# A two-layer hybrid trunk on one core: the norms' inverse root on GpSimd, later transposes, low parts by accumulating DMAs, and a shared end

## The chip, the cores and the metric

The kernel runs on one core of a Trainium2 chip. The metric is the time of one execution on the device in microseconds (us). The engines are named as in the profile: PE is TensorE's matmul, PEld its weight load, DVE is VectorE, ACT is ScalarE, POOL is GpSimd, SP is SyncE, whose queue starts most of the DMAs. "Issue" means that an engine's queue starts a DMA, "landing" that its last byte is written.

## The reference

The input `x` is 512 tokens of 1024 numbers in float32. Two layers follow each other; each has a token mixer and a gated feed-forward part, and each of these four parts ends in a residual sum and a layer norm:

```python
for i in range(DEPTH):                                  # DEPTH = 2
    if i % 3 == 0: y = gla_mixer(h, ...)                # gated linear attention (layer 0)
    elif i % 3 == 1: y = gdn_mixer(h, ...)              # gated DeltaNet (layer 1)
    h = layer_norm(ALPHA * h + y, ln_g[i, 0], ln_b[i, 0])
    h = layer_norm(ALPHA * h + conv_ffn(h, ...), ln_g[i, 1], ln_b[i, 1])

def layer_norm(x, g, b):
    mu = mean(x, -1); var = mean(square(x - mu), -1)
    return (x - mu) * rsqrt(var + 1e-5) * g + b

def conv_ffn(x, w_in, conv_w, w_out):                   # w_in: 1024 x 5632, w_out: 2816 x 1024
    gate, up = split(causal_dwconv(x @ w_in, conv_w), 2)
    return (gelu(gate, approximate=False) * up) @ w_out
```

## The kernel before

All matrix products are made in three terms: each operand is split into a high part in the format fp32r and a low part, the remainder, and TensorE adds high x high, high x low and low x high (`tm_terms`, and `fm_mms` for products whose result lies transposed). The high part of a weight is a cast on ACT (`wsh`, `wh`), the low part a subtraction on DVE (`wsl<-raw,wsh`, `wl<-raw,wh`). For some weights (`plan_fm(..., bydma=True)`) the low part is instead made by ACT, which writes minus the rounded weight, and by a DMA from POOL's queue that adds the raw weight to it (L315 to L317).

The tokens are four blocks of 128 (`tb` 0 to 3). The residual stream is kept as eight tiles `h[tb][hf]` of 128 tokens by 512 features, the halves `hf` 0 and 1. At the end of each of the four parts, a block's projection adds to `h`, `bn_stats` takes the statistics of both halves, and the norm follows: `ln_stats` makes the mean and variance (`ln_mv`, `ln_var`), a first guess of the inverse root by integer arithmetic on its bits (the seed, L680), and three Newton rounds of two steps each (L683, L684: `ln_t`, `ln_rs`). `ln` then makes `ln_nb` = -mean x root, scales one half on ACT (L697) and the other on DVE (L698), and TensorE transposes both (`tr4`, `xT`, L172). ACT takes the transposed tiles out with the norm's factors (`xf`), and they are split in high and low parts (`xh`, `xl`) that the next part's products read. There are 16 such norms: four blocks after GLA's output projection, after the first FFN, after GDN's output projection and at the end. The last four go through `ln_out` instead, which applies the norm's factors by two DVE operations per half (L747, L748) and writes the output by SP's queue.

An FFN computes its output projection in parts: most of it in Strassen-like sums while the input products run, and the rest, the last 512 of the 2816 rows, in `last_proj`: eight weights of 128 x 512 held in slots (`wsh`, `wsl`), eight output tiles (`tm`) of four chunks, three products each. The fourth chunk's other operand is the last gate times up value of the FFN, which ACT casts to `gh` and DVE completes to `gl`.

The program is written out as one stream for all engines. `clk` is a planner's count of TensorE's time, `vec` one of DVE's; tasks (`spawn`, `pump`) are resumed when `clk` reaches their due time, so that work of one block is put between the products of another. The instructions of an engine keep the scheduler's order; what `keep_in_program_order` is given stays where it is written. Raw weights go through three buffers (`RAWB = 3`), loaded by SP's queue in the order of a plan; a buffer can be loaded anew when whoever reads it has finished. `look` sets how many weights ahead are cast; the letter `l` in an FFN's `order` raises it for the last projection's weights:

```python
self.fm_items(items, steps, order[:-4] + "l" + order[-4:] if plain else order)
```

Of the kernel before, what the change touches and what calls it, by code (L numbers as in the profile page):

```python
# [8 lines left out]
F32 = mybir.dt.float32  # L9
# [3 lines left out]
AF = mybir.ActivationFunctionType  # L13
ALU = mybir.AluOpType

P = 128
D = 1024
S = 512
# [23 lines left out]
INV_DELAY = 18.0  # L42
CONV_DELAY = 6.0
COLS_DELAY = 64.0
BASE_PACE = 1.8
# [7 lines left out]
def blk(i, n=P):  # L53
    return slice(i * n, i * n + n)


class Trunk:
# [97 lines left out]

    def mm(self, out, a, b, start=True, stop=True, open_group=False):
        n = 1
        for d in b.shape[1:]:
            n *= d
        self.clk += n * (0.00045 if b.dtype == F32R else 0.00175)  # L160
        t = self.nc.tensor.matmul(out, a, b, start=start, stop=stop, skip_group_check=open_group)  # L161
        if self.pin:
            self.tc.keep_in_program_order(t)
# [5 lines left out]

    def tr(self, out, a, n=P):  # L170
        self.clk += 0.11
        t = self.nc.tensor.transpose(out, a, self.ident[:n, :n])  # L172
        if self.pin:
            self.tc.keep_in_program_order(t)

    def tr4(self, out, a):
        for j in range(4):
            self.tr(out[:, blk(j)], a[:, blk(j)])

# [92 lines left out]
    def issue(self, item):  # L272

        nc = self.nc
# [27 lines left out]
        if self.in_slots(item):  # L302
            w = []
            for j in range(used // S):
                wh, wl = self.slot("wsh", F32R), self.slot("wsl", F32R)
                nc.scalar.copy(wh, raw[:, blk(j, S)])
                nc.vector.tensor_sub(wl, raw[:, blk(j, S)], wh)
                self.vec(0.7)
                w.append((wh, wl))
            return w  # L310
# [115 lines left out]

    def tm_terms(self, ps, ah, al, wh, wl, first, last):
        self.mm(ps, ah, wh, first, False)
        self.mm(ps, ah, wl, False, False)
        self.mm(ps, al, wh, False, last)  # L430

# [238 lines left out]
    def ln_stats(self, tb):  # L670
# [11 lines left out]
        for _ in range(3):  # L682
            nc.vector.scalar_tensor_tensor(t, rs, hv, rs, ALU.mult, ALU.mult)  # L683
            nc.vector.scalar_tensor_tensor(rs, t, 1.5, rs, ALU.subtract, ALU.mult)  # L684
        self.vec(2.0)
        return mv, rs

    def ln(self, tb, spill=False):
# [10 lines left out]
        ready = self.vec(0.65)  # L699
        yield ready - self.clk + 0.2  # L700
        for hf in range(2):
            ps = self.psum("xT")
            self.tr4(ps, h[hf])
            xf = self.slot("xf")
# [37 lines left out]
    def ln_out(self, tb, out):  # L742
        nc = self.nc
        gb, h = self.ln_gb(), self.h[tb]
        mv, rs = self.ln_stats(tb)
        for hf in range(2):
            nc.vector.scalar_tensor_tensor(h[hf], h[hf], mv[:, 0:1], gb[hf], ALU.subtract, ALU.mult)  # L747
            nc.vector.scalar_tensor_tensor(h[hf], h[hf], rs, gb[2 + hf], ALU.mult, ALU.add)  # L748
            nc.sync.dma_start(out[blk(tb), blk(hf, S)], h[hf])
        yield 0.0  # L750
# [31 lines left out]
    def ffn_plan(self, w_in, w_out):  # L782
# [10 lines left out]
        for hf in range(2):  # L793
            for f in range(2 * p0, 2 * p1, 2):
                self.plan_tm(w_out, f * P, 2, hf * S, True)

# [21 lines left out]
    def ffn(self, cw, li, g, b, final, out=False):  # L818
# [3 lines left out]
        for p0, p1 in CHUNKS + (PLAIN,):  # L822
# [3 lines left out]
            for f in range(2 * p0, 2 * p1):  # L826
# [17 lines left out]
                items += [gate, up]  # L844
            self.fm_items(items, steps, order[:-4] + "l" + order[-4:] if plain else order)
            steps = self.sums_proj(xs, p0 == 0)
# [7 lines left out]
    def last_proj(self, xs, final):  # L854
# [739 lines left out]
```

## Time and profile before

| | us |
|---|---|
| three runs | 1286.13, 1277.92, 1284.02 |
| their median | 1284.02 |
| profiled execution | 1284.87 |
| its span, first to last instruction | 1283.2 |
| PE busy in it | 1258.0 (98%) |
| DVE busy | 872.2 (68%) |
| ACT busy | 611.3 (48%) |
| POOL busy | 152.2 (12%) |
| mean granted TensorE clock | 0.984 of full speed |

The span is what the trace covers; the device's time is 1.7 us longer. An engine's share is its busy time over the span. In the rows below, a timeline row has the start in us, the duration, the engine, the line, the operation with out<-in, and in brackets the idle time before it with its releaser. A row of waits has the engine and line that waited, the one that released it, the total, the number of waits and the longest. A row of a group has the count, then the busy time and the mean in ns. A row of DMA issues has the queue, the count, the size of each and the median us from issue to landing. A row of a stretch has its bounds, its length, the busy time of PE, PEld, DVE, ACT and POOL with the number of instructions, and at its end the granted clock, the DMA share and GB/s.

### The profile page before, as it was taken

The numbers are of one execution on the slowest core, as the hardware profiler recorded it, in microseconds if no ns is written. First come the engines' busy times: TensorE is split into PE (matmuls) and PEld (weight loads), VectorE is DVE, ScalarE is ACT, GpSimd is POOL, SyncE is SP. The second block draws the span as 40 slices with busy tenths as digits, with TensorE's granted clock in tenths as the row PEclk, the third lists the DMA queues.
The fourth block names the chain that finished last, engine by engine and source line by source line (L and its number), as shares of the span: only waits on it lengthen the run. The fifth ranks groups of instructions, "written<-read, shape, count | busy, mean of one in ns | idle before, by whom it ended". The sixth has DMA issues, their size and how long they took to land.

```text
span 1283.2 us, 17783 instructions
## 1 busy us (share of the span) xinstructions
PE 1258.0 (98%) x6558; PEld 1060.1 (83%) x6558; DVE 872.2 (68%) x1704; ACT 611.3 (48%) x1176; POOL 152.2 (12%) x226
## 2 busy tenths in 40 slices
PE   8999999999999999999999999999999999999996
PEld 6878888988888888879888889988898888888885
DVE  3683366578666666686789925668877766766678
ACT  3553443644544444435765525544554554554440
POOL 4000000012201201101112210100002211211200
PEclk9999999999999999999999959999999999999998
DMA  6422224078757757641444411333239766766821
GB/s 183 116 69 65 66 95 136 17 155 214 170 127 182 162 128 176 148 134 66 128 125 110 125 37 35 99 103 95 82 99 212 159 157 160 161 153 150 211 82 65
DMA packets 182646, 159.07 MB, mean 124 GB/s; under 512 B 18328, under 2 KB 141786, under 8 KB 182560
## 3 DMA queue, kind: packets, MB, share of 16 engines
q1 hardware_dynamic: 161728, 114.05, 30.1%
q0 software_dynamic: 19440, 42.06, 17.8%
q10 hardware_dynamic: 1392, 1.84, 0.4%
q8 instruction: 51, 0.84, 0.3%
q14 instruction: 35, 0.29, 0.1%
HBM read 141.65 MB, written 5.78 MB: 115 GB/s over the span
## 4 chain that ended last, share of the span: by engine, by line
PE 82%; DVE 7%; DMA 2%; ACT 1%; issue 1%; SPq 0%; DVEq 0%; ACTq 0%; POOLq 0%
PE fm L161 43%; PE tm L161 29%; PE o L161 2%; PE R L161 1%; PE V L161 1%; DMA wq<-in_ffn_w_out_dram 1%; PE xT L172 1%; DVE conv L1166 1%; DVE wl L322 1%; PE pg L161 1%; PE vn L161 1%; PE yT L172 1%; PE qkT L172 1%; PE s L161 0%; PE qs L161 0%
## 5 line engine op out<-in xcount | busy, mean ns | idle before, releaser
L161 PE MATMUL fm<-xh,wh 128*128 128x512 f32 (+1 forms) x1104 | 409.2, 371 | 0.4 <-ACT wh L321 0.4
L161 PE MATMUL fm<-xl,wh 128*128 128x512 f32 (+1 forms) x1104 | 405.5, 368 | 0.0
L161 PE MATMUL fm<-xh,wl 128*128 128x512 f32 (+1 forms) x1096 | 401.7, 368 | 2.4 <-DVE wl L322 2.4
L322 DVE TENSOR_TENSOR wl<-raw,wh 128x1024 fp32r<-128x1024 f32 (+1 forms) x134 | 162.6, 1215 | 142.1 <-ACT wh L321 139.0
L161 PEld LDWEIGHTS fm<-xh,wh 128*128 128x128 f32 x1104 | 209.6, 190 | 34.2 <-ACT wh L321 1.2
L161 PEld LDWEIGHTS fm<-xh,wl 128*128 128x128 f32 x1096 | 207.8, 190 | 36.3 <-DVE wl L322 3.0
L161 PEld LDWEIGHTS fm<-xl,wh 128*128 128x128 f32 x1104 | 209.8, 190 | 32.7
L321 ACT CAST wh<-raw 128x1024 fp32r<-128x1024 f32 (+1 forms) x134 | 139.7, 1043 | 200.8 <-PE fm L161 107.9
L815 DVE SCALAR_TENSOR_TENSOR conv<-fm,ffn_cw,conv 128x511 f32<-128x511 f32 (+1 forms) x176 | 131.1, 746 | 16.5 <-ACT conv L813 14.5
L266 ACT CAST wh<-wq 128x512 fp32r<-128x512 f32 x126 | 74.7, 619 | 110.9 <-DMA wq<-in_ffn_w_out_dram 37.5
L267 DVE TENSOR_TENSOR wl<-wq,wh 128x512 fp32r<-128x512 f32 x126 | 84.9, 687 | 61.8 <-ACT wh L266 61.3
L224 POOL DMA_DIRECT2D wq<-in_ffn_w_out_dram x72 | 63.0, 901 | 263.2 <-DVE wl L267 150.2
L161 PE MATMUL tm<-wh,gh 128*128 128x512 f32 x216 | 84.4, 391 | 0.3 <-DVE h L521 0.3
L161 PE MATMUL tm<-wl,gh 128*128 128x512 f32 x216 | 84.2, 390 | 0.0
L161 PE MATMUL tm<-wh,gl 128*128 128x512 f32 x216 | 84.2, 390 | 0.0
L161 PE MATMUL tm<-wh,xh 128*128 128x512 f32 x192 | 79.6, 415 | 1.0 <-ACT qk L982 1.0
L161 PE MATMUL tm<-wh,xl 128*128 128x512 f32 x192 | 75.5, 393 | 0.0
L161 PE MATMUL tm<-wl,xh 128*128 128x512 f32 x192 | 75.2, 391 | 0.0
L317 POOL DMA_DIRECT2D wl<-raw x20 | 17.5, 875 | 442.0 <-ACT wl L316 425.4
L521 DVE TENSOR_TENSOR h<-h,tm 128x512 f32<-128x512 f32 x68 | 44.9, 683 | 34.8 <-PE tm L161 34.8
L813 ACT ACTIVATE conv<-fm,ffn_cw 128x512 f32<-128x512 f32 x88 | 59.7, 681 | 0.0
L1166 DVE SCALAR_TENSOR_TENSOR conv<-fm,gdn_cw,conv 128x509 f32<-128x509 f32 (+2 forms) x72 | 53.4, 744 | 4.6 <-ACT conv L1164 4.1
(297 smaller groups left out, 1877.4 us busy)
## 6 DMA issues: line engine op xcount, KB each, us to landing
raw<-in_ffn_w_in_dram SPq DMA_DIRECT2D x88, 512.0 KB, 4.9
wq<-in_ffn_w_out_dram SPq DMA_DIRECT2D x72, 256.0 KB, 5.9
wq<-in_ffn_w_out_dram POOLq DMA_DIRECT2D x72, 256.0 KB, 5.2
raw<-in_gdn_w_in_dram SPq DMA_DIRECT2D x32, 512.0 KB, 4.1
raw<-in_gla_w_in_dram SPq DMA_DIRECT2D x23, 512.0 KB, 3.7
wl<-raw POOLq DMA_DIRECT2D x20, 512.0 KB, 4.8
raw<-in_gla_w_out_dram SPq DMA_DIRECT2D x8, 512.0 KB, 3.7
h<-in_ln_b_dram POOLq DMA_DIRECT2D x16, 256.0 KB, 7.3
```

What stands on the lines that cost most here:

```text
L161: t = self.nc.tensor.matmul(out, a, b, start=start, stop=stop, skip_group_check=open_group)
L172: t = self.nc.tensor.transpose(out, a, self.ident[:n, :n])
L224: nc.gpsimd.dma_start(t[i], quad(i, r, col), accum_op=ALU.add)
L266: nc.scalar.copy(wh, t)
L267: nc.vector.tensor_sub(wl, t, wh)
L317: nc.gpsimd.dma_start(wl.bitcast(F32), raw, accum_op=ALU.add)
L321: nc.scalar.copy(wh[:, cols], raw[:, cols])
L322: nc.vector.tensor_sub(wl[:, cols], raw[:, cols], wh[:, cols])
L521: nc.vector.tensor_tensor(h, h, banks[bank][j], op)
L813: nc.scalar.activation(a, ps, AF.Identity, scale=tap(2))
L815: nc.vector.scalar_tensor_tensor(a[:, d:], ps[:, :S - d], tap(2 - d), a[:, d:], ALU.mult, ALU.add)
L1166: self.conv = nc.vector.scalar_tensor_tensor(a[:, d:], ps[:, :S - d], tap(3 - d), a[:, d:], ALU.mult, ALU.add)
```

## The change

Three parts. The norms: the three Newton rounds go to GpSimd, as three operations each instead of two; the planner counts 0.5 instead of 2.0 for DVE; a norm's transposes become due `LN_LAG` = 2.7 after DVE's planned end instead of 0.2, and are pinned in program order, as are the last projection's products (`tr`, `tr4` and `tm_terms` hand the new argument `order` on to `mm`'s condition). The last projection: the low parts of its weights are made by ACT and an accumulating DMA of POOL's queue; the lookahead is raised eight letters before the end of `order` instead of four. The end: for blocks 0 and 1, `ln_out` normalises on ACT, multiplies on DVE and adds `ln_b` by an accumulating DMA.

```diff
+LN_LAG = 2.7
...
-    def mm(self, out, a, b, start=True, stop=True, open_group=False):
+    def mm(self, out, a, b, start=True, stop=True, open_group=False, order=False):
...
-        if self.pin:
+        if self.pin or order:
             self.tc.keep_in_program_order(t)
...
     def issue(self, item):
...
                 nc.scalar.copy(wh, raw[:, blk(j, S)])
-                nc.vector.tensor_sub(wl, raw[:, blk(j, S)], wh)
-                self.vec(0.7)
+                if item[5] > 1:
+                    nc.scalar.mul(wl, raw[:, blk(j, S)], -1.0)
+                    nc.gpsimd.dma_start(wl.bitcast(F32), raw[:, blk(j, S)], accum_op=ALU.add)
+                else:
+                    nc.vector.tensor_sub(wl, raw[:, blk(j, S)], wh)
+                    self.vec(0.7)
...
     def ln_stats(self, tb):
...
         for _ in range(3):
-            nc.vector.scalar_tensor_tensor(t, rs, hv, rs, ALU.mult, ALU.mult)
-            nc.vector.scalar_tensor_tensor(rs, t, 1.5, rs, ALU.subtract, ALU.mult)
-        self.vec(2.0)
+            nc.gpsimd.tensor_mul(t, rs, rs)
+            nc.gpsimd.tensor_scalar(t, t, hv, 1.5, op0=ALU.mult, op1=ALU.subtract)
+            nc.gpsimd.tensor_mul(rs, rs, t)
+        self.vec(0.5)
...
     def ln(self, tb, spill=False):
...
-        yield ready - self.clk + 0.2
+        yield ready - self.clk + LN_LAG
         for hf in range(2):
             ps = self.psum("xT")
-            self.tr4(ps, h[hf])
+            self.tr4(ps, h[hf], True)
...
     def ln_out(self, tb, out):
...
         mv, rs = self.ln_stats(tb)
+        if tb < 2:
+            nb = self.small([P, 1], "ln_nb")
+            nc.vector.scalar_tensor_tensor(nb, mv[:, 0:1], -1.0, rs, ALU.mult, ALU.mult)
+            for hf in range(2):
+                nc.scalar.activation(h[hf], h[hf], AF.Identity, bias=nb, scale=rs)
+                nc.vector.tensor_mul(h[hf], h[hf], gb[hf])
+                nc.gpsimd.dma_start(h[hf], self.gb_rows[1][blk(hf, S)].partition_broadcast(P), accum_op=ALU.add)
+                nc.sync.dma_start(out[blk(tb), blk(hf, S)], h[hf])
+            return
         for hf in range(2):
             nc.vector.scalar_tensor_tensor(h[hf], h[hf], mv[:, 0:1], gb[hf], ALU.subtract, ALU.mult)
...
     def ffn_plan(self, w_in, w_out):
...
-                self.plan_tm(w_out, f * P, 2, hf * S, True)
+                self.plan_tm(w_out, f * P, 2, hf * S, 2)
...
     def ffn(self, cw, li, g, b, final, out=False):
...
-            self.fm_items(items, steps, order[:-4] + "l" + order[-4:] if plain else order)
+            self.fm_items(items, steps, order[:-8] + "l" + order[-8:] if plain else order)
...
     def last_proj(self, xs, final):
...
-                    self.tm_terms(ps, *(t[:, blk(tb)] for t in xs[c]), *ws[hf][c], c == 0, c == n - 1)
+                    self.tm_terms(ps, *(t[:, blk(tb)] for t in xs[c]), *ws[hf][c], c == 0, c == n - 1, True)
```

In the changed kernel the lines stand some further down: TensorE's products are at L162 and its transposes at L173, the Newton steps at L688 to L690, `ln_nb` at L702, the scalings at L703 and L704. Three places of the order follow, a row for an instruction, with its line, operation, out<-in and what it waits for.

DVE behind GDN's output projection, before: the seed of block 1 (`ln_rs_8208`) and the end of both blocks' Newton rounds, with `ln_nb` and the scaling of block 0 between them.

```order
L680 TENSOR_SCALAR ln_rs_8208<-ln_var_8206 128x1 [waits DVE_49]
L684 SCALAR_TENSOR_TENSOR ln_rs_8165<-ln_t_8166,ln_rs_8165 128x1 [waits DVE_49]
L683 SCALAR_TENSOR_TENSOR ln_t_8209<-ln_rs_8208,ln_var_8206 128x1 [waits DVE_49]
L696 SCALAR_TENSOR_TENSOR ln_nb_8174<-ln_mv_8161,ln_rs_8165 128x1 [waits DVE_49]
L698 TENSOR_SCALAR h_7863<-h_7863,ln_mv_8161,ln_rs_8165 128x512
```

DVE at the same place in the changed kernel, from block 0's seed (`ln_rs_8197`) to block 1's scaling (`h_7897`).

```order
L685 TENSOR_SCALAR ln_rs_8197<-ln_var_8195 128x1 [waits DVE_49]
L474 SCALAR_TENSOR_TENSOR h_7907<-h_7907,tm_8116 128x512 [waits PE_49]
L702 SCALAR_TENSOR_TENSOR ln_nb_8209<-ln_mv_8193,ln_rs_8197 128x1 [waits Pool_49]
L704 TENSOR_SCALAR h_7895<-h_7895,ln_mv_8193,ln_rs_8197 128x512
L481 BN_STATS ln_st_8093<-h_7907 128x6 [waits DVE_49]
L678 BN_AGGR ln_mv_8239<-ln_st_8093 128x2 [waits DVE_49]
L680 TENSOR_SCALAR ln_var_8241<-ln_mv_8239 128x1 [waits DVE_49]
L685 TENSOR_SCALAR ln_rs_8243<-ln_var_8241 128x1 [waits DVE_49]
L702 SCALAR_TENSOR_TENSOR ln_nb_8255<-ln_mv_8239,ln_rs_8243 128x1 [waits Pool_49]
L704 TENSOR_SCALAR h_7897<-h_7897,ln_mv_8239,ln_rs_8243 128x512
```

Block 1's statistics and seed moved from before block 0's `ln_nb` to behind it, and each `ln_nb` now waits for POOL.

PE at the same place, before: the second half of block 0 (`h_7873`), and the products up to block 1's first half (`h_7865`).

```order
L172 MATMUL xT_8257<-ident_80,h_7873 128x128 [waits Activation_49]
L172 MATMUL xT_8257<-ident_80,h_7873 128x128 x3
L161 MATMUL tm_8086<-wsh_7997,yh_7739 128x512
L161 MATMUL tm_8086<-wsl_7998,yh_7739 128x512
L161 MATMUL tm_8086<-wsh_7997,yl_7740 128x512
L161 MATMUL tm_8086<-wsh_8001,yh_7739 128x512
L161 MATMUL tm_8086<-wsl_8002,yh_7739 128x512
L161 MATMUL tm_8086<-wsh_8001,yl_7740 128x512
L172 MATMUL xT_8294<-ident_80,h_7865 128x128 [waits DVE_49]
```

PE there in the changed kernel, where the two halves are `h_7905` and `h_7897`.

```order
L162 MATMUL tm_8117<-wsh_8135,yl_7975 128x512
L173 MATMUL xT_8295<-ident_80,h_7905 128x128 [waits Activation_49]
L173 MATMUL xT_8295<-ident_80,h_7905 128x128 x3
L173 MATMUL xT_8307<-ident_80,h_7897 128x128 [waits DVE_49]
L173 MATMUL xT_8307<-ident_80,h_7897 128x128 x3
L162 MATMUL tm_8118<-wsh_8029,yh_7771 128x512
```

The six products that stood between the two halves now stand behind both; the transposes of blocks 2 and 3 moved to later places.

ACT at the end of the first FFN, before: the last of its weights' casts, then casts of GDN's first weights (`wh`) around `gh`.

```order
L306 CAST wsh_4713<-raw_4711 128x512 [waits DMAHW7_49]
L306 CAST wsh_4717<-raw_4711 128x512
L813 ACTIVATE conv_4774<-fm_4743,ffn_cw_28_176 128x512 [waits PE_49]
L321 CAST wh_4739<-raw_4737 128x1024 [waits DMAHW0_49]
L321 CAST wh_4770<-raw_4768 128x1024 [waits DMAHW1_49]
L563 CAST gh_4779<-conv_4774 128x512 [waits DVE_49]
L321 CAST wh_4797<-raw_4795 128x1024 [waits DMAHW2_49,PE_49]
L321 CAST wh_4811<-raw_4809 128x1024 [waits DMAHW3_49,PE_49]
```

ACT there in the changed kernel.

```order
L307 CAST wsh_4726<-raw_4724 128x512 [waits DMAHW7_49]
L309 ACTIVATE wsl_4727<-raw_4724 128x512
L307 CAST wsh_4731<-raw_4724 128x512
L309 ACTIVATE wsl_4732<-raw_4724 128x512
L828 ACTIVATE conv_4736<-fm_4659,ffn_cw_28_176 128x512 [waits PE_49]
L326 CAST wh_4759<-raw_4757 128x1024 [waits DMAHW0_49,PE_49,Activation_49]
L844 ACTIVATE conv_4736<-conv_4736 128x512 [waits DVE_49,Activation_49]
L326 CAST wh_4790<-raw_4788 128x1024 [waits DMAHW1_49,PE_49]
L828 ACTIVATE conv_4794<-fm_4763,ffn_cw_28_176 128x512 [waits PE_49]
L326 CAST wh_4817<-raw_4815 128x1024 [waits DMAHW2_49,PE_49]
L326 CAST wh_4831<-raw_4829 128x1024 [waits DMAHW3_49,PE_49]
L568 CAST gh_4799<-conv_4794 128x512 [waits DVE_49]
```

`gh` moved behind the third and fourth of GDN's casts, and each weight of the projection has a second ACT operation.

More of the change, by code (lines that the diff above doesn't have):

```diff
@@ L168, in vec, with tr, tr4 @@
         return self.dve
-    def tr(self, out, a, n=P):
+    def tr(self, out, a, n=P, order=False):
         self.clk += 0.11
         t = self.nc.tensor.transpose(out, a, self.ident[:n, :n])
-        if self.pin:
+        if self.pin or order:
             self.tc.keep_in_program_order(t)
-    def tr4(self, out, a):
+    def tr4(self, out, a, order=False):
         for j in range(4):
-            self.tr(out[:, blk(j)], a[:, blk(j)])
+            self.tr(out[:, blk(j)], a[:, blk(j)], order=order)
     def mm4(self, out, a, b):
@@ L424, in fm_items, with tm_terms @@
             raise RuntimeError
[L427 to L430, printed above, removed]
+    def tm_terms(self, ps, ah, al, wh, wl, first, last, order=False):
+        self.mm(ps, ah, wh, first, False, order=order)
+        self.mm(ps, ah, wl, False, False, order=order)
+        self.mm(ps, al, wh, False, last, order=order)
     def tm_half(self, a, n, tail, done, slots=False):
```

## The prediction

> **What bounds the kernel now.** I read the page's busy times first, then TensorE's waits, then the timeline around each wait the change touches, then the rows that price the new work.
>
> ```profile
> span 1283.2 us, 17783 instructions
> PE 1258.0 (98%) x6558; PEld 1060.1 (83%) x6558; DVE 872.2 (68%) x1704; ACT 611.3 (48%) x1176; POOL 152.2 (12%) x226
> ```
>
> TensorE is busy for 98% of the span, so only two things can alter the time: its idle moments, and what follows its last product. No product is added or removed, so the work on DVE, ACT and POOL counts only where TensorE waits for it. Of TensorE's waits, each row naming who released it, with the total, the number and the longest:
>
> ```profile
> PE xT L172 <- DVE h L698: 2.8, 2, 2.7
> PE xT L172 <- DVE ln_rs L684: 0.7, 1, 0.7
> PE tm L161 <- ACT gh L563: 0.3, 1, 0.3
> ```
>
> These three rows are the change's ground: a norm's transposes waiting for the normalised half, and the last projection waiting for an operand that ACT casts. They add up to 3.8 us, so removing every one of them would give 0.3% of the span. The largest stall, on the timeline:
>
> ```profile
> 574.78 0.39 PE L161 MATMUL tm<-wsh,gl 128*128 128x512 f32 x1
> 577.26 0.54 DVE L698 TENSOR_SCALAR h<-h,ln_mv,ln_rs 128x512 f32<-128x512 f32 x1
> 577.86 1.09 PE L172 MATMUL xT<-ident,h 128*128 128x128 f32 x8 [2.69 <-DVE h L698]
> ```
>
> From start to start this is 3.08 us, where a product's successor normally starts 0.23 later (563.28 to 563.51 in rows below): 2.85 us lost at the first norm after the first FFN.
>
> **The price of a Newton step.** On DVE alone, the six steps run from the first row to the second:
>
> ```profile
> 586.53 0.22 DVE L683 SCALAR_TENSOR_TENSOR ln_t<-ln_rs,ln_var 128x1 f32<-128x1 f32 x1
> 587.88 0.16 DVE L696 SCALAR_TENSOR_TENSOR ln_nb<-ln_mv,ln_rs 128x1 f32<-128x1 f32 x1
> ```
>
> That is 1.35 us for six. The change makes nine on GpSimd, each waiting for the one before. The trace has no GpSimd arithmetic on one column, so I bound it:
>
> ```profile
> L1282 POOL TENSOR_SCALAR_AFFINE_SELECT dt<-dt 128x512 f32<-128x512 f32 x8 | 5.2, 646 | 116.4 <-DVE dt L1280 116.4
> masks.py:199 POOL TENSOR_SCALAR_AFFINE_SELECT ident<-ident 128x128 f32<-128x128 f32 x1 | 0.3, 287 | 0.0
> L1580 POOL MEMSET const-float32-1.0<- 128x1 f32 x1 | 0.1, 98 | 0.0
> 15.69 0.30 POOL L952 MEMSET maskf<- 64x256 f32 x1
> 16.06 0.61 POOL L954 CAST gla_mask<-maskf 128x512 uint8<-128x512 f32 x1
> ```
>
> The select takes 646 ns for 512 columns and 287 for 128; a line through both leaves 167 ns for none. A one-column fill takes 98. The cast that depends on the fill at 15.69 starts 0.07 after that fill's end. So a dependent step costs at least 0.10 + 0.07 = 0.17, at most the whole 128-column select, 0.29 + 0.07 = 0.36. I take 0.167 + 0.07 = 0.24, since the select reads and calculates as these steps do. Nine are 2.16 us, some 2.3 with the two changes of engine, against 1.35. The Trainium skill, "GPSIMD Engine Reference", section 3.1, measures an elementwise add on GpSimd at 1.96 times DVE's; by that ratio, as an estimate, a step is 0.44 us and the sum would be some 22 us larger, but the 98 ns fill speaks against it, and the page's measurement is of 2048 columns, not one.
>
> **Who stands behind it.** DVE executes in order, and the changed order puts `ln_nb`, which now waits for POOL, ahead of DVE's other work. Before, a Newton's steps were interleaved with the next block's adds and statistics; now DVE stands still through each chain. The third norm, behind GDN's output projection, before:
>
> ```profile
> 908.70 0.15 DVE L680 TENSOR_SCALAR ln_rs<-ln_var 128x1 int32<-128x1 int32 x1
> 909.74 0.69 DVE L476 BATCH_NORM_STATS2 ln_st<-h 128x6 f32<-128x512 f32 x1
> 910.47 0.21 DVE L673 BATCH_NORM_AGGREGATE ln_mv<-ln_st 128x2 f32<-128x12 f32 x1
> 911.25 0.15 DVE L696 SCALAR_TENSOR_TENSOR ln_nb<-ln_mv,ln_rs 128x1 f32<-128x1 f32 x1
> 912.00 0.63 PE L172 MATMUL xT<-ident,h 128*128 128x128 f32 x4 [0.66 <-DVE ln_rs L684]
> 912.38 0.47 PE L161 MATMUL tm<-wsh,yh 128*128 128x512 f32 x1
> 912.94 0.54 DVE L698 TENSOR_SCALAR h<-h,ln_mv,ln_rs 128x512 f32<-128x512 f32 x1
> 913.85 0.60 PE L172 MATMUL xT<-ident,h 128*128 128x128 f32 x4
> ```
>
> Block 0: the seed at 908.70 ends at 908.85; 2.3 us of chain put `ln_nb` at 911.15 against 911.25, so its transposes start as before, to 0.1 us. Block 1 then starts late: its statistics (0.69 + 0.21 and two steps of 0.15, with gaps of some 0.06: 1.4) stand behind block 0's `ln_nb` and scaling (0.6), and its chain of 2.3 follows: its own `ln_nb` comes near 911.15 + 0.6 + 1.4 + 2.3 = 915.45, its scaling at 915.55 instead of 912.94, and the half is ready at 916.1. TensorE, whose transposes of block 1 now stand directly behind the second half of block 0's, is there after six products (912.38 to 913.85) and four transposes (0.36), at 914.2. New stall: **1.9 us**. Blocks 2 and 3 gain up to 0.4 from standing behind more products. This place: **+1.5** (from -2 with steps of 0.17, to +6 with 0.36, where all four chains are bare).
>
> Behind GLA's projection the order of all three engines is the same, but DVE has no weights' low parts and residuals between; **+0.6** there (-0.7 to +4, by the same ends).
>
> **The last projection of the first FFN.** The low parts leave DVE, the raw buffers are freed later, and a cast changes its place:
>
> ```profile
> 554.24 0.68 DVE L307 TENSOR_TENSOR wsl<-raw,wsh 128x512 fp32r<-128x512 f32 x1
> 558.82 1.15 ACT L306 CAST wsh<-raw 128x512 fp32r<-128x512 f32 x2 [2.21 <-DMA raw<-in_ffn_w_out_dram]
> 563.28 0.39 PE L161 MATMUL tm<-wsh,gh 128*128 128x512 f32 x1
> 563.51 0.39 PE L161 MATMUL tm<-wsl,gh 128*128 128x512 f32 x1
> 565.16 0.61 ACT L563 CAST gh<-conv 128x512 fp32r<-128x512 f32 x1
> 565.82 0.50 PE L161 MATMUL tm<-wsh,gh 128*128 128x512 f32 x1 [0.34 <-ACT gh L563]
> 566.03 1.05 ACT L321 CAST wh<-raw 128x1024 fp32r<-128x1024 f32 x1 [0.27 <-DMA raw<-in_gdn_w_in_dram]
> raw<-in_gdn_w_in_dram SPq DMA_DIRECT2D x32, 512.0 KB, 4.1
> wl<-raw POOLq DMA_DIRECT2D x20, 512.0 KB, 4.8
> hd<-h POOLq DMA_DIRECT2D x8, 256.0 KB, 2.6
> ```
>
> The fourth load of these weights goes out when the first raw buffer is free. Before, that was DVE's second subtraction (ended 554.92), and the load landed at 558.82. Now it is the landing of two accumulating DMAs; but the earlier raise of the lookahead lets ACT start the casts as soon as the first load is there, so I put the landing 2 us earlier, at 556.8 (0 to 3 are possible). Four ACT operations of 0.57 end at 559.1. The last accumulation moves 256 KB within SBUF: between the 2.6 of a spill and the 4.8 of twice the size, I take 3.7; it lands at 562.8. Only then can SP load the next GDN weight into that buffer (4.1): 566.9. ACT casts two such weights (1.05 each) and only behind them, where before they stood behind it, `gh`: 566.9 + 2.1 + 0.61 = 569.6. TensorE asks for `gh` at 565.3, nine products of 0.23 after 563.28; I add 0.3 for the handovers. New stall: **4.6 us**, in place of the 0.5 there (565.82 against 565.3). The 2.85 at 574.78 goes: DVE is rid of eight subtractions of 0.69, 5.5 us, and the stall itself lets it catch up. This place: 4.6 - 0.5 - 2.85 = **+1.2** (landings of 2.6 and 4.8: -1 and +3.5).
>
> The second FFN's end has no next layer's weights in front of `gh`:
>
> ```profile
> 1250.69 0.62 ACT L563 CAST gh<-conv 128x512 fp32r<-128x512 f32 x1 [3.00 <-DVE conv L834]
> ```
>
> ACT had 3.00 us to spare there; eight more operations of 0.57 use 4.6, partly beside loads: **+0.6** (0 to 1.7).
>
> **The end.** Last product, last block's seed, and its final steps:
>
> ```profile
> 1271.38 0.39 PE L161 MATMUL tm<-wsh,gl 128*128 128x512 f32 x1
> 1276.41 0.15 DVE L680 TENSOR_SCALAR ln_rs<-ln_var 128x1 int32<-128x1 int32 x1
> 1278.48 1.42 DVE L748 SCALAR_TENSOR_TENSOR h<-h,ln_rs,gb 128x512 f32<-128x512 f32 x2
> h<-in_ln_b_dram POOLq DMA_DIRECT2D x16, 256.0 KB, 7.3
> ```
>
> Four long operations of blocks 0 and 1 leave DVE for ACT. Their outputs now wait in SP's queue for an accumulation of 7.3, and the outputs of blocks 2 and 3 stand behind them; but block 1's last product ends four halves of twelve products before 1271.38, at 1260.6, so statistics (2), chain (2.3), ACT (1.6), DVE (0.7) and the accumulation end by 1275.5, some 4 us before block 3's. I count the seed 0.8 us earlier and the chain with its handovers 2.3 where 2.07 passed (1276.41 to 1278.48), less one scaling that lies inside it: **-0.4** (-3 to +4).
>
> Sum: 0.6 + 1.2 + 0.6 + 1.5 - 0.4 = **+3.5**. The profiled execution took 1284.87, its span and 1.7 around it; that gives 1288.4. The median of the three runs shown is 0.85 lower, so I say **1288**. Above 0.24, some 108 steps (12 of the 16 chains) lie bare, 1.1 us for each 0.01 of a step; below, about 0.85, since TensorE is then covered.
>
> **Rivals.** *Cheap steps.* At 0.17 a chain is 1.6 us, near DVE's own 1.35, DVE is really relieved and the norms' stalls go: -6 from my sum, so 1279 to 1283. It decides at 0.20. For it: the 98 ns fill. Against it: these steps read two operands. Chance 0.2.
>
> *Dear steps,* the slower side with the largest weight: at 0.30 or above, 108 x 0.06 = 6.5 to 108 x 0.12 = 13 more, 1294 to 1302. For it: the 128-column select, and DVE operations that may lie beside a chain. By the Trainium skill, "SBUF — State Buffer", section "SBUF: two separate sides", a DVE operation with two SBUF inputs and a GpSimd operation that reads SBUF exclude each other for a whole instruction; one 0.69 us subtraction in some four chains would, as an estimate, add 2 to 3 us; no run here shows it. Chance 0.17.
>
> *The clock.*
>
> ```profile
> 565.00:600.00 35.00, 31.98 (x186) 27.29 (x185) 28.93 (x77) 18.53 (x42) 6.17 (x10) 1.00 0.36 109
> 748.00:779.00 31.00, 31.00 (x347) 25.87 (x346) 11.10 (x27) 7.19 (x19) 0.63 (x1) 0.62 0.12 36
> ```
>
> The granted clock (third figure from the right) stayed at 1.00 through the 2.69 us of idling at 575, but was 0.62 for 31 us elsewhere. If 4.6 us of idling bring that on at 570, 31 us at 0.62 lose up to 12: 1296 to 1300. Chance 0.08. The Trainium skill, "TensorE: Matmul & The Clock Gate", part 1, has the clock halved after an idle window of some 3.4 us; the 1.00 above agrees, its idling being shorter.
>
> *No stall at `gh`*: the accumulations land in 2.6, or the casts start later than I think but off the path: 1282 to 1285. Chance 0.05. The forecast, 1284 to 1292: 0.5.
>
> **Range and chances.** 1% of 1284 is 12.8 us, about what a measurement of this kernel can tell from no change. 8 in 10 needs the forecast, most of the cheap steps and half of the dear: 1279 to 1301. Below 1271.2 nothing in these cases reaches (0.03 for what I don't see, such as the low clock after 748 falling away). Above 1296.9 lie over half of the dear steps and half of the clock's case, with a little for a later `gh`: 0.18. Within 1%: 0.79.
>
> **What would show it.** Nine POOL rows a norm, 0.24 apart; DVE's `ln_nb` waiting on POOL; one TensorE wait of 4 to 5 us for `gh` near 565 with no wait for `h` at 575; two waits of one to two us after 909; `wsl<-raw` landing in about 3.7; last product to end about as long as now. I am wrong if steps are 0.17 or 0.30 apart, if `gh` is in time, or if the clock falls after 570.

## The result, and the profile after

The changed kernel took 1311.2 us (median of 4 runs, 1309.09 to 1313.09) against 1284.13 before: **1.0239 times as long, 95% interval 1.0207 to 1.0270**. The forecast was 1288, its range ended at 1301. The profiled execution of the changed kernel took 1313.09.

Span and busy times, from its page:

```profile
span 1311.4 us, 17884 instructions
PE 1260.2 (96%) x6558; PEld 1059.3 (81%) x6558; DVE 848.2 (65%) x1590; ACT 622.4 (47%) x1196; POOL 205.3 (16%) x390
```

PE's busy time is 2.2 us more than before's 1258.0, and the span 28.2 us more: the loss is TensorE's waiting, and what follows its last product. DVE did get lighter, by 24 us; but for the one old wait of 2.7 us for `h`, nobody was waiting for that. TensorE's waits:

```profile
PE tm L162 <- ACT gh L568: 12.2, 2, 10.6
PE xT L173 <- DVE h L704: 7.5, 6, 2.1
PE fm L162 <- DVE xh L717: 2.4, 2, 1.5
PE fm L162 <- DVE xl L721: 1.6, 5, 0.3
```

Before, `gh` had 0.3, and the transposes `xT` 3.5 together. One single wait of 10.6 us for `gh` and a handful of one to two us for the norms have taken their place.

To see where the time went, I set the two traces side by side at events that both have: the first product of GLA's output projection (211.00 us before), of the first FFN's output (314.19), GDN's first transpose `qkT` (613.49), the first product of GDN's output projection (896.22), of the second FFN's output (1000.35), and the last product's start (1271.38). The difference in each stretch, in us against before's profile, for the changed kernel and for all twelve experiments, one column by its number in the next section:

| stretch | change | 1 | 2 | 3 | 4 | 5 | 6 | 7 | 8 | 9 | 10 | 11 | 12 |
|---|---|---|---|---|---|---|---|---|---|---|---|---|---|
| to GLA's projection | -1.0 | -0.6 | -0.2 | 1.3 | -0.7 | -0.8 | -1.0 | -2.0 | -1.0 | -1.0 | -1.0 | 1.8 | -0.9 |
| norms behind GLA | **3.8** | 6.3 | 0.0 | 1.2 | 0.0 | 16.1 | 8.4 | 0.0 | 0.0 | 4.7 | 0.0 | 0.0 | -0.4 |
| first FFN's end and norms | **11.2** | 3.9 | 8.7 | -2.3 | -0.2 | 12.9 | 6.0 | 5.1 | 13.7 | 3.3 | 2.5 | -2.4 | 9.2 |
| GDN up to its projection | -1.5 | -1.5 | -1.5 | -7.2 | 1.3 | -9.8 | -0.4 | -10.1 | 1.5 | -5.7 | -1.7 | -11.5 | -7.0 |
| norms behind GDN | **6.8** | 10.6 | -0.3 | 0.3 | 0.1 | 18.2 | 10.3 | -1.0 | -0.1 | 8.4 | -0.5 | -0.2 | -0.4 |
| second FFN to last product | **1.6** | -0.2 | 2.1 | -0.6 | 0.1 | 0.0 | -0.2 | -0.1 | 2.1 | -0.6 | 0.6 | -0.6 | 3.7 |
| last product to the end | **7.3** | 6.6 | -0.1 | -0.1 | -0.2 | 16.2 | 6.7 | 0.0 | 1.5 | 6.6 | 0.0 | -0.2 | -0.3 |

The fourth row is not the change's doing: it moves by 11 us between kernels that are the same there (see the last section). It is why a single execution's time can mislead by more than most of these parts are worth, and why the experiments are read by place as well as by their times.

**The steps.** The groups of Newton steps on GpSimd, and one round as the timeline has it:

```profile
L689 POOL TENSOR_SCALAR ln_t<-ln_t,ln_var 128x1 f32<-128x1 f32 x48 | 14.7, 307 | 4.8
L688 POOL TENSOR_TENSOR ln_t<-ln_rs 128x1 f32<-128x1 f32 x48 | 11.0, 228 | 261.6 <-DVE ln_rs L685 259.1
L690 POOL TENSOR_TENSOR ln_rs<-ln_rs,ln_t 128x1 f32<-128x1 f32 x48 | 9.2, 191 | 4.0
```

```profile
224.12 0.20 POOL L688 TENSOR_TENSOR ln_t<-ln_rs 128x1 f32<-128x1 f32 x1
224.42 0.29 POOL L689 TENSOR_SCALAR ln_t<-ln_t,ln_var 128x1 f32<-128x1 f32 x1
224.79 0.19 POOL L690 TENSOR_TENSOR ln_rs<-ln_rs,ln_t 128x1 f32<-128x1 f32 x1
225.06 0.19 POOL L688 TENSOR_TENSOR ln_t<-ln_rs 128x1 f32<-128x1 f32 x1
```

A round is 0.94 us (224.12 to 225.06), so a step is **0.31** on average, not 0.24, and a chain of nine 2.8 instead of 2.16. The gap from step to step, 0.08 to 0.10, is near what I took (0.07); the step with a value per partition and a constant costs 0.29 on a single column, where I had read 0.167 from the select.

**Behind GDN's projection.** Two of TensorE's waits there, and what ACT and DVE did before the second (some rows left out):

```profile
929.29 0.66 PE L173 MATMUL xT<-ident,h 128*128 128x128 f32 x4 [2.14 <-DVE h L704]
...
933.13 1.21 ACT L713 ACTIVATE xf<-xT,lb,lg 128x128 f32<-128x128 f32 x3
936.34 0.16 DVE L702 SCALAR_TENSOR_TENSOR ln_nb<-ln_mv,ln_rs 128x1 f32<-128x1 f32 x1 [2.33 <-POOL ln_rs L690]
936.87 0.42 DVE L717 CAST xh<-xf 128x512 fp32r<-128x512 f32 x1
937.35 0.38 PE L162 MATMUL fm<-xh,wh 128*128 128x256 f32 x1 [1.47 <-DVE xh L717]
```

The first is block 1's half, for which the prediction has a stall of 1.9. The second is another place: `xf` is complete at 934.34, but DVE stands still for 2.33 us at `ln_nb` of block 2, and block 1's `xh`, which the second FFN's first products need, stands behind it.

**The wait for `gh`.** ACT, the last of the projection's weights, then `gh` (in order of time, some rows left out):

```profile
561.66 0.62 ACT L307 CAST wsh<-raw 128x512 fp32r<-128x512 f32 x1 [5.78 <-DMA raw<-in_ffn_w_out_dram]
...
574.92 1.04 ACT L326 CAST wh<-raw 128x1024 fp32r<-128x1024 f32 x1 [5.32 <-DMA raw<-in_gdn_w_in_dram]
577.08 1.04 ACT L326 CAST wh<-raw 128x1024 fp32r<-128x1024 f32 x1 [1.11 <-DMA raw<-in_gdn_w_in_dram]
578.03 0.61 ACT L568 CAST gh<-conv 128x512 fp32r<-128x512 f32 x1
```

The chain has the links that the prediction named, each later: the fourth load of the projection's weights has landed at 561.66 (I had 556.8), the weights of GDN at 574.9 and 577.1 (566.9), `gh` is ready at 578.6 (569.6). The fourth load, issued at 555.44, and the last accumulation, issued at 564.15, took from issue to landing:

```profile
raw<-in_ffn_w_out_dram SPq DMA_DIRECT2D x1, 512.0 KB, 6.2
wsl<-raw POOLq DMA_DIRECT2D x1, 256.0 KB, 6.2
```

The granted clock across that wait, from a view of stretches:

```profile
570.00:577.00 7.00, 0.00 (x0) 0.00 (x0) 3.87 (x6) 1.04 (x1) 0.95 (x1) 0.67 0.75 159
577.00:580.00 3.00, 1.30 (x3) 1.07 (x4) 2.15 (x4) 1.56 (x2) 0.00 (x0) 0.50 0.44 110
580.00:583.00 3.00, 3.00 (x9) 2.29 (x9) 1.80 (x3) 0.00 (x0) 0.00 (x0) 0.55 0.55 143
583.00:586.00 3.00, 3.00 (x15) 2.47 (x14) 1.62 (x4) 0.00 (x0) 0.00 (x0) 1.00 0.32 97
```

The third figure from the right falls to 0.50 and is back at 1.00 from 583. The nine products that start from 578.70 on take until 582.69, 3.99 us, where nine at 0.23 take 2.07: 1.9 us lost on top of the wait.

**The end.** DVE behind the last product (which starts at 1292.26):

```profile
1296.72 1.41 DVE L763 SCALAR_TENSOR_TENSOR h<-h,ln_rs,gb 128x512 f32<-128x512 f32 x2 [2.04 <-POOL ln_rs L690]
1298.65 0.67 DVE L884 TENSOR_TENSOR h<-h,tm 128x512 f32<-128x512 f32 x1
1301.06 0.15 DVE L685 TENSOR_SCALAR ln_rs<-ln_var 128x1 int32<-128x1 int32 x1
1304.48 1.42 DVE L763 SCALAR_TENSOR_TENSOR h<-h,ln_rs,gb 128x512 f32<-128x512 f32 x2 [2.62 <-POOL ln_rs L690]
```

Block 3's last sum (1298.65) stands behind block 2's final operations, which wait for block 2's chain. So two chains lie one behind the other, and block 3's seed comes 8.8 us after the last product; before it was 5.0.

### The profile page after: what moved, and what is told of

It is laid out like the page before. It is cut to its first block, busy times and chain, and to the rows that moved or that the text cites. A ratio compares the mean times of both kernels' runs of the same rounds, so it can differ in the third digit from the quotient of the medians.

```text
span 1311.4 us, 17884 instructions
## 1 busy us (share of the span) xinstructions
PE 1260.2 (96%) x6558; PEld 1059.3 (81%) x6558; DVE 848.2 (65%) x1590; ACT 622.4 (47%) x1196; POOL 205.3 (16%) x390
## 5 line engine op out<-in xcount | busy, mean ns | idle before, releaser
L162 PE MATMUL fm<-xh,wh 128*128 128x512 f32 (+1 forms) x1104 | 409.3, 371 | 2.7 <-DVE xh L717 2.4
L162 PE MATMUL fm<-xl,wh 128*128 128x512 f32 (+1 forms) x1104 | 405.3, 367 | 1.6 <-DVE xl L721 1.6
L162 PE MATMUL fm<-xh,wl 128*128 128x512 f32 (+1 forms) x1096 | 401.2, 367 | 2.1 <-DVE wl L327 2.1
L162 PEld LDWEIGHTS fm<-xh,wh 128*128 128x128 f32 x1104 | 209.2, 190 | 37.5 <-DVE xh L717 3.2
L162 PEld LDWEIGHTS fm<-xl,wh 128*128 128x128 f32 x1104 | 209.4, 190 | 35.3 <-DVE xl L721 2.6
L162 PEld LDWEIGHTS fm<-xh,wl 128*128 128x128 f32 x1096 | 207.5, 190 | 36.3 <-DVE wl L327 2.7
L162 PE MATMUL tm<-wh,gh 128*128 128x512 f32 x216 | 84.1, 389 | 0.0
L162 PE MATMUL tm<-wh,gl 128*128 128x512 f32 x216 | 84.0, 389 | 0.0
L162 PE MATMUL tm<-wl,gh 128*128 128x512 f32 x216 | 84.0, 389 | 0.0
L162 PE MATMUL tm<-wh,xh 128*128 128x512 f32 x192 | 79.6, 414 | 1.0 <-ACT qk L997 1.0
L162 PE MATMUL tm<-wh,xl 128*128 128x512 f32 x192 | 75.4, 393 | 0.0
L162 PE MATMUL tm<-wl,xh 128*128 128x512 f32 x192 | 75.1, 391 | 0.0
L688 POOL TENSOR_TENSOR ln_t<-ln_rs 128x1 f32<-128x1 f32 x48 | 11.0, 228 | 261.6 <-DVE ln_rs L685 259.1
```

Source lines behind the costliest of these rows:

```text
L688: nc.gpsimd.tensor_mul(t, rs, rs)
```

## The experiments

Each was compared with before on its own chip, where before's median was 1278 to 1279.

**1. Newton alone.** The kernel before with only this:

```diff
-            nc.vector.scalar_tensor_tensor(t, rs, hv, rs, ALU.mult, ALU.mult)
-            nc.vector.scalar_tensor_tensor(rs, t, 1.5, rs, ALU.subtract, ALU.mult)
+            nc.gpsimd.tensor_mul(t, rs, rs)
+            nc.gpsimd.tensor_scalar(t, t, hv, 1.5, op0=ALU.mult, op1=ALU.subtract)
+            nc.gpsimd.tensor_mul(rs, rs, t)
```

> The kernel before with only the Newton rounds on GpSimd; planner, transposes, low parts and end as before. Theory (each chain of nine dependent GpSimd steps takes 2.8 us, and DVE stands still through it with TensorE behind it): the three sets of norms lose 4 to 7 us each against before where 3.8, 3 and 6.8 were lost in the full change, the end 3 to 7 more: 1296 to 1304. Rival (the transposes' new places make the loss, the chains are hidden beside other work): within 3 us of before.

1309.67 against 1278.02: 1.0237 (1.0210 to 1.0263). TensorE's waits:

```profile
PE xT L172 <- DVE h L699: 15.9, 8, 3.3
```

The theory holds and was too low: the chains alone cost 27 us by place (6.3 + 3.9 + 10.6 + 6.6), and the ratio to before is that of the whole change. Of the end's 7.3 in the full change, 6.6 appear here without the shared end.

**2. Low parts alone.** The kernel before with the diff of `issue`, `ffn_plan` and the lookahead's place.

> The kernel before with only the last projections' low parts by ACT and an accumulating DMA, and the earlier raise of the lookahead. Theory (TensorE waits some 10 us for gh at the first FFN's end, since gh stands behind two casts of GDN weights whose loads wait for the last accumulations to land): one wait of 9 to 11 us for gh, the old 2.7 us wait for h gone, 2 us more at the second FFN's end and 1 to 2 from the clock falling: 1291 to 1297. Rival (gh was late in the full change because the norms' GpSimd work or pinned products delayed it): gh at most 3 us late, 1281 to 1286.

1294.2 against 1278.02: 1.0120 (1.0093 to 1.0148).

```profile
PE tm L161 <- ACT gh L567: 11.9, 2, 9.7
```

The theory holds: 9.7 us at the first FFN with no GpSimd chain in the program, +8.7 at that place net of the old wait for `h`, +2.1 at the second FFN. The earlier raise of the lookahead is part of this run; it was not run by itself.

**3. Places alone.** The kernel before with the lag of 2.7 and the pinned order.

> The kernel before with only the transposes' lag of 2.7 and the pinned order; Newton on DVE with the planner's cost as before. Theory: the places alone cost nothing, since the two old waits for h (2.8 and 0.7 us) get shorter with more products ahead of the transposes: 1280 to 1285. Rival (pinning a block's transposes directly behind another's makes the waits after GDN's and GLA's projections): two or more waits of over 1 us for h or xh there, 1288 to 1296.

1278.43 against 1278.02: 0.9996 (0.9976 to 1.0016). No wait for `h` above 0.2 us is left; 2.3 us are gained at the first FFN and 1.2 lost behind GLA. By time, the places cost nothing.

**4. The end alone.** The kernel before with the new branch of `ln_out`.

> The kernel before with only the shared end: blocks 0 and 1 normalised on ACT, multiplied on DVE, ln_b by an accumulating DMA; Newton on DVE. Theory (the end's loss of 7 us in the full change comes from two bare chains in series and is not the sharing's): the time from the last product to the end stays within 1.5 us of before's 11.8: 1282 to 1287. Rival (the accumulations of 7 us hold back the outputs in SP's queue, or the last DMA's end is late): the end 3 us longer or more, 1287 to 1292.

1277.58 against 1278.02: 0.9991 (0.9967 to 1.0015), and 11.6 us from the last product to the end where before had 11.8. Sharing the end is free, and gains nothing.

**5. Six rounds.** Experiment 1 with the rounds doubled. (The seed is negative and each round turns the sign, so that after six rounds the root is negative and every norm's result is wrong; the remark on digits in the expectation does not hold, the instructions are as it says.)

```diff
-        for _ in range(3):
+        for _ in range(6):
             nc.gpsimd.tensor_mul(t, rs, rs)
```

> Newton on GpSimd as in the run of Newton alone, with six rounds instead of three (the extra rounds change the result only in its last digits). Theory (the chain's length lies on the path at nearly every one of the 16 norms, since DVE, in order, stands still behind it): nine more steps of 0.31 are 2.8 us for each norm, 12 to 16 of them bare: 34 to 45 us more than the run of Newton alone, 1343 to 1355 against a before of 1284, by place about 8 to 11 at each of the four. Rival (the loss is a fixed cost of handing over to GpSimd and back, or of the changed order of DVE's work): under 15 us more.

1339.38 against 1278.0: 1.0461 (1.0425 to 1.0498), 29.7 above experiment 1. By time that is under the 34 to 45 of the theory, and far over the rival's 15. By place the second three rounds add 9.8, 9.0, 7.6 and 9.6: 36 us, which GDN's faster stretch in that execution hid in part. At 2.8 us a chain that is 12.8 of 16 chains bare, that is, waited for in full; the prediction had counted 12.

**6. DVE kept free.** Experiment 1 with -mean x root on GpSimd and both halves scaled on ACT:

```diff
-        nc.vector.scalar_tensor_tensor(nb, mv[:, 0:1], -1.0, rs, ALU.mult, ALU.mult)
-        nc.scalar.activation(h[1], h[1], AF.Identity, bias=nb, scale=rs)
-        nc.vector.tensor_scalar(h[0], h[0], mv[:, 0:1], rs, op0=ALU.subtract, op1=ALU.mult)
+        nc.gpsimd.tensor_scalar(nb, mv[:, 0:1], rs, -1.0, op0=ALU.mult, op1=ALU.mult)
+        for hf in range(2):
+            nc.scalar.activation(h[hf], h[hf], AF.Identity, bias=nb, scale=rs)
```

> Newton on GpSimd as in the run of Newton alone; -mean x root is made on GpSimd too, and both halves are scaled on ACT, so that DVE waits for no chain except at the end, where the norm is as before. Theory (it is DVE's standing still that costs, not the chain's own 2.8 us): the places behind GLA's and GDN's projections fall from +6 and +10 to under +3 and +5, the end's +6.6 stays: 14 to 20 us above before. Rival (the chain's latency alone, with one more step and ACT's second 0.82, holds the transposes back just as much): 25 us above before or more.

1308.13 against 1278.0: 1.0225 (1.0189 to 1.0262).

```profile
PE xT L172 <- ACT h L699: 18.5, 7, 4.0
```

Here my theory fell and the rival held: DVE waits for no chain at these places, and 8.4, 6.0 and 10.3 us are lost, together no less than in experiment 1. So the loss does not need DVE's standing still: the chain's own length between a block's statistics and its transposes is enough, here with a tenth step and ACT's second scaling on it. Since the run makes the chain longer as it frees DVE, it does not show that DVE's standing still costs nothing. Behind GDN, block 1's chain starts at 925.02, as block 0's ends, so there GpSimd itself was a second queue in which block 1 waited; at the other norms 1.8 us or more lie between two chains.

**7. Four raw buffers.** Experiment 2 with more buffers, and slots given up for them:

```diff
-SLOTS = 53
-RAWB = 3
+SLOTS = 51
+RAWB = 4
```

> Low parts by accumulating DMA as in the run of them alone, with four raw buffers instead of three and two slots fewer to make room; the order of every engine's casts is the same, only the loads' waits change. Theory (gh is late because loads wait for accumulations to land before a buffer is free): the fourth load lands some 4 us earlier and the last GDN load waits for an earlier accumulation: the wait for gh falls from 9.7 to 3 to 5 us, and 5 to 7 us of the run's loss go. Rival (the accumulations crowd the DMA queues and every load is slow): the wait for gh stays over 7 us.

1279.12 against 1278.0: 1.0027 (0.9995 to 1.0058).

```profile
PE tm L161 <- ACT gh L567: 6.6, 1, 6.6
```

Between the two: the wait falls from 9.7 to 6.6, not to 3 to 5. By place 5.1 are still lost where 8.7 were. The time flatters it: six executions took 1277 to 1280 and four 1287 to 1289, and in the profiled one, of the shorter, GDN's stretch was 10.1 shorter than in before's profile. The buffers are part of the cause. The rest stands in the time to landing of single transfers: accumulations, the first and the last three, and the first of GDN's loads, issued among them:

```profile
wsl<-raw POOLq DMA_DIRECT2D x1, 256.0 KB, 3.3
wsl<-raw POOLq DMA_DIRECT2D x2, 256.0 KB, 7.8
wsl<-raw POOLq DMA_DIRECT2D x1, 256.0 KB, 8.6
raw<-in_gdn_w_in_dram SPq DMA_DIRECT2D x1, 512.0 KB, 11.5
```

The first is issued at 545.9 and lands in 3.3. Of eight in a row, the last of them some 1.04 apart, each takes longer, and the last (553.5) lands 8.6 after its issue. The load, issued at 550.96, takes 11.5 where the median before was 4.1, the next one 10.0: what the rival said of the loads holds for these two.

**8. `gh` ahead of the weights.** Experiment 2 with a smaller raise of the lookahead:

```diff
             if kind == "l":
-                self.look = TAIL + WB
+                self.look = TAIL
```

> Low parts by accumulating DMA as in the run of them alone, but the raised lookahead is four weights instead of eight, so that gh is cast ahead of the last two weights of the projection and of three of GDN's. Theory (it is gh's place behind GDN's casts that stalls TensorE): no wait for gh over 1 us; but the projection's last low parts now land later, so a wait of 0 to 4 us for a low part or its cast may take its place: 4 to 9 us below the run of low parts alone. Rival (accumulations land too late for the projection itself wherever gh stands): 2 us below it at most.

1302.16 against 1278.0: 1.0169 (1.0141 to 1.0196), worse than experiment 2 by 8, as only the rival allows. No wait for `gh` is left, but others came:

```profile
PE tm L161 <- DMA wsl<-raw: 4.7, 2, 3.1
PE xT L172 <- DVE h L702: 4.1, 2, 3.9
PE tm L161 <- ACT wsh L306: 3.9, 1, 3.9
```

The casts of the last four of the eight weights moved behind `gh` too, and behind a cast of GDN's that waits 5.4 us for its load, and TensorE waits for these weights instead. Moving one cast ahead does not help while the accumulations themselves are late.

**9. A longer lag.** Experiment 1 with the pinned places, due 6.0 behind DVE's planned end (and the planner's 0.5, as in the change).

> Newton on GpSimd with the transposes pinned as in the full change, but due 6.0 instead of 2.7 behind DVE's planned end; low parts and end as before. Theory (a chain's latency costs only where TensorE has too few products of its own to put in front of the transposes): behind GLA's, the first FFN's and GDN's projections together 8 to 13 us are lost, where Newton alone lost 20.8; the end stays at +6.6, since nothing follows it: 14 to 20 above before. Rival (the next part's first products wait for the same norms, so a later place only moves the wait from the transposes to xh and xl): 18 or more lost at the three places.

1303.43 against 1279.12: 1.0187 (1.0149 to 1.0226).

```profile
PE fm L162 <- DVE xh L713: 10.9, 3, 4.3
PE xT L173 <- DVE h L700: 2.4, 1, 2.4
```

16.4 us lost at the three places: between theory and rival, nearer the rival; by time 24 above before, over the 14 to 20 expected. The wait moved from the transposes to `xh`, which the next part's first products need. Behind GLA and GDN the full change with its lag of 2.7 lost 10.6, this run with 6.0 loses 13.1, and experiment 1 with the old 0.2 and no pins lost 16.9. Of these three, 2.7 is the best and hides a third; the runs differ in more than the lag, so no optimum is shown.

**10. Half of the low parts.** Experiment 2 with only the first four weights by DMA:

```diff
-                self.plan_tm(w_out, f * P, 2, hf * S, 2)
+                self.plan_tm(w_out, f * P, 2, hf * S, 1 if hf else 2)
```

> Low parts by accumulating DMA for the first four of the last projection's eight weights of 128x512 only, the other four by DVE as before; the lookahead raised early as in the run of all eight. Theory (eight accumulations 1.04 us apart queue up behind each other, so that they land 3.3, 3.7, 4.4 and up to 8.8 us after issue, and crowd the loads of raw weights): the four land in 3.3 to 4.5, the last load of the projection in 4 to 5 instead of 6.4, and the wait for gh falls from 9.7 to 2 to 4 us. Rival (gh's place behind two casts of GDN weights alone makes the wait): still over 7 us.

1284.75 against 1279.12: 1.0032 (1.0005 to 1.0059).

```profile
PE tm L161 <- ACT gh L567: 3.5, 2, 2.9
wsl<-raw POOLq DMA_DIRECT2D x4, 256.0 KB, 3.7
```

The wait for `gh` is 2.9, as the theory has it. At the first FFN the four land in 3.7 at the median, but the last of them takes 5.8 and the projection's last load 5.2, both over what was expected. `gh`'s place behind two casts is the same as in experiment 2, so that place alone is worth 2.9 at most.

**11. A version from what paid.** Newton and low parts on DVE, the lag and pins only behind the first FFN, the shared end:

```diff
-        yield ready - self.clk + LN_LAG
+        yield ready - self.clk + (LN_LAG if spill else 0.2)
...
-            self.tr4(ps, h[hf], True)
+            self.tr4(ps, h[hf], spill)
```

> A version made from what the runs showed to pay: Newton and low parts on DVE as before; the lag of 2.7 and pinned transposes only for the norms behind the first FFN, where the run of the places alone gained 2.3 us; the last projection's products pinned; the shared end, which cost nothing. If the gains by place add up: no wait for h at the first FFN, 2 to 3 us below before, a ratio of 0.998. Rival: they are lost again in the part that follows: within 1 us of before.

1278.21 against 1279.12: 0.9981 (0.9958 to 1.0004). At its place it gains the 2.4 us, and no wait for `h` is left there; the time agrees with 0.998, and does not prove it.

**12. All but Newton.** The full change with the two old DVE steps in the loop.

> The full change with the Newton rounds back on DVE as in the kernel before; the planner's costs, the lag of 2.7, the pinned order, the low parts by DMA and the shared end as changed. Theory (by place, GpSimd's chains cost the full change 3.8 behind GLA, some 2.5 behind the first FFN, 6.8 behind GDN and 7.3 at the end, and the rest is the low parts): behind GLA and GDN at most 1 us each is left, the end is back at 11 to 13 us, the wait for gh stays at 10 to 11: 8 to 12 above before, 17 to 22 below the full change. Rival (the parts work on each other, so that without the chains gh is in time, or the later places cost without them): a wait for gh under 6 us, or over 3 us lost behind GLA or GDN.

1292.14 against 1278.03: 1.0120 (1.0087 to 1.0154).

```profile
PE tm L162 <- ACT gh L568: 12.9, 2, 10.8
```

The theory holds by place: nothing is lost behind GLA and GDN, the end is back at 11.5, and the wait for `gh` is there as it was; with 3.7 instead of 2.1 at the second FFN, the total is 2 above what I expected. So by place GpSimd's chains are about 19 us of the full change (15 by the two ratios) and the low parts 11 to 13. The chains' part is smaller than alone (27); that the later places hide the difference is likely, and not shown by a run of these two alone.

## Why the prediction was wrong

The bottleneck was read rightly: TensorE's waits and the end moved the time, DVE's relief was worth no more than the one old wait that went with it, and the shared end was free. The mechanisms named were there too, but four terms of the sum were mis-sized. The profiled execution lies 28.2 us above before's, the sum had 3.5. Of the 24.7 between them, 10.0 are the first FFN's end, 8.5 the norms behind GLA and GDN, 7.7 the end of the program and 1.0 the second FFN; the other stretches were 2.5 shorter.

- **The price of a step.** 0.24 was taken, from the row it seemed nearest to, and 0.31 measured. The bounds of 0.17 and 0.36 held. "Dear steps" with a chance of 0.17 came true for the step. Its slope of 108 bare steps was near (experiment 5: 115), and 0.07 x 108 is, as an estimate, 7.6 us of the error, which would bring the forecast to 1296; the rest has other reasons. A round took 0.22 more than three steps of 0.24; 0.12 of it is the step with a value per partition, for which the select without one did not stand, and the rest the products at 0.19 and the longer gaps. The 0.44 of the other estimate would bring the sum near the measured time, but the step was not 0.44.
- **Behind GLA and GDN.** +0.6 and +1.5 forecast, +3.8 and +6.8 measured. The one stall that I worked out in full, block 1 behind GDN, came out: 1.9 forecast, 2.14 measured (`xT` at 929.29). In part that is luck: counted from block 0's seed, the half was ready 0.9 later than forecast, and TensorE came to it 0.5 later. The step that failed is "blocks 2 and 3 gain up to 0.4". Block 3's transposes waited 1.52, and block 2's chain held DVE, so that the next part's first products waited for `xh` (1.47) and twice for `xl` (0.3 each), a wait that the sum does not have. DVE's standing still was followed only to the transposes, and not to the other work behind it; nor is it needed for the loss, as experiment 6 shows.
- **The wait for `gh`.** 4.6 forecast, 10.6 measured, and +11.2 instead of +1.2 at the place. `gh` was ready 9.0 later than forecast, and TensorE asked for it 2.7 later, since the program was 2.8 behind by then. The step that failed is the landings: each transfer got the time of a row from another place. The first six accumulations took 3.3 to 6.7, and the fourth load, issued among them, 6.2 where it took 3.8 before. In experiment 2, where nothing is late before this place, that load went out 2.5 earlier than before, as I had it, and landed at 558.8, as before. The last accumulation took 6.2 instead of 3.7. It did not stand in a row of eight: when it and the one ahead of it were issued (563.1 and 564.2), the first six had landed and two loads of GDN's weights were under way; which of these transfers slowed it was not tried. Then the second of the two loads behind it took 6.0 instead of 4.1.
- **The clock.** The rival with a chance of 0.08 came about in the smaller form: 10.6 us of idling, half clock for the first 4 us after it, 1.9 us lost; not 31 us at 0.62. The Trainium skill, "TensorE: Matmul & The Clock Gate", part 1, has the clock halved after an idle window of some 3.4 us and restored after one busy window of that length: the traces agree with both (2.69 us of idling left it at 1.00, and 4 us of products brought it back).
- **The end.** -0.4 forecast, +7.3 measured. I took block 3's seed as free to come 4.2 us after the last product. But DVE's order has block 3's sums behind block 2's wait, so two chains are in series where the working had one. This is the same "who is queued behind the waiting instruction" that I followed behind GDN and left out here.

The three rows of the old waits, 3.8 us, were the change's whole possible gain at these places. The places alone took 2.3 of it (experiment 3); the other two parts added waits that were larger than what there was to win.

## What to carry to other kernels

Before a chain of tiny operations goes to another engine, price the whole chain there, from the end of the statistics to the first reader, and not the load that it takes off: here 1.35 us on DVE became 2.8 on GpSimd, bare at some 13 of 16 norms by experiment 5, to relieve an engine that was busy 68% of the time. A DMA's time to landing, taken from rows of other places, is no price for one that runs among others (3.3 for the first accumulation, 6.2 to 8.6 for the last here), and where a buffer is freed only by such a landing, every load behind it moves. Where an engine executes in order, ask at each new wait which work of the *next* block stands behind it, at the end of the program too, and for every reader of that work and not only the first.

## What the runs showed of the hardware

- One-column operations on GpSimd cost 0.19 us (product of two tiles) and 0.29 (with a value per partition and a constant), 0.27 to 0.37 from start to start when each waits for the one before.
- A GpSimd step beside a DVE operation with two SBUF inputs takes longer. On the changed kernel's timeline:

```profile
230.65 0.69 DVE L721 TENSOR_TENSOR xl<-xf,xh 128x512 fp32r<-128x512 f32 x1
230.88 0.61 POOL L689 TENSOR_SCALAR ln_t<-ln_t,ln_var 128x1 f32<-128x1 f32 x1
```

  0.61 instead of 0.29, ending 0.15 after DVE's. This agrees with the exclusion that the Trainium skill states in "SBUF — State Buffer", section "SBUF: two separate sides". Six of the 144 steps took 0.44 us or more, all beside a long DVE operation, five of these with two SBUF inputs. So over all steps it is small: means of 228 and 307 ns against medians of 194 and 291, some 2.4 us in 48 rounds.
- GDN's stretch of small products (from `V` to `s`) took 35.5 to 48.3 us in the profiles, with the same instructions and no longer waits, at granted clocks of 0.90 and 0.61 (rows of experiments 11 and 4):

```profile
734.90:770.40 35.50, 35.04 (x521) 30.10 (x522) 16.88 (x38) 13.78 (x42) 7.97 (x15) 0.90 0.24 54
734.60:782.90 48.30, 47.96 (x520) 41.13 (x521) 16.98 (x38) 13.92 (x42) 8.02 (x15) 0.61 0.19 40
```

  It is by far the largest difference between two executions outside the places that the change touches, up to 13 us. What decides it was not tried and stays open.
